# Fewer TensorE instructions in a cross-covariance attention kernel: one transpose for V of two units, fp32 transposes of 128 columns for the logits, grams of two units in the same PSUM banks

## Chip, cores, metric

One core of one Trainium2 chip. Times are device microseconds (us) of one execution; a profile belongs to one execution and gives its span, which is about 1.7 us shorter than the time reported for the same run. Every comparison uses runs of the fast state (a run counts as slow when it is more than 1.5% above the fastest of the same kernel) unless the text says otherwise. Ratios are the mean time of one kernel's fast runs over the mean of the other's fast runs of the same rounds, so they are not quite the ratio of the medians that are quoted beside them; intervals are 95%.

## The reference

```python
# Q, K, V: (8 batches, 12 heads, 512 rows, 64 columns), float32
Q_norm = Q / (np.linalg.norm(Q, axis=-2, keepdims=True) + 1e-10)
K_norm = K / (np.linalg.norm(K, axis=-2, keepdims=True) + 1e-10)
attn = np.einsum('bhnd,bhne->bhde', Q_norm, K_norm)          # 64 x 64 a head
attn = np.exp(attn - np.max(attn, axis=-1, keepdims=True))
attn = attn / (np.sum(attn, axis=-1, keepdims=True) + 1e-10)
return np.einsum('bhnd,bhde->bhne', V, attn)
```

37.75 MB are read and 12.58 MB written.

## The kernel before

Four heads are a *unit*: 128 partitions, 32 for each head, with 16 rows of 64 columns in each partition. There are 24 units and 12 *pairs* of units. A unit's Q and K stand side by side as bf16; one product of this tile with itself (the *gram*, 64 matmuls) gives K^T Q and, on its diagonal, the squares of all norms. V is transposed on TensorE, copied to SBUF, and multiplied with the normalised exponentials. A planner in the program (`Order`) decides the order in which the pieces are issued; all engines then work through their queues in that order.

```python
def cast_v(eng, u):
    vb[u] = vbp.tile([128, T, D], BF16, name="vb")            # one tile a unit
    copy(eng, vb[u], v32[u])

def grams(u):
    g = gram[u] = ps_g.tile([128, HU, 512], F32, name="gram") # four banks, one unit
    for t in range(T):                                        # T = 16
        for h in range(HU):                                   # HU = 4
            x = qkb[u][32 * h:32 * (h + 1), t, :]
            nc.tensor.matmul(g[:, h, 0:2 * D], x, x, start=(t == 0), stop=(t == T - 1))

def powers(s):                                                # pair s
    # ... r8 = (sums of squares) ** -0.5 on GpSimd
    nc.gpsimd.tensor_tensor(
        out=t_, in0=kq[s], in1=r8[s][:, HU:, None].to_broadcast([128, HU, D]), op=ALU.mult)

def logits(s):
    l = lg[s] = ps_l.tile([128, HU, D], F32, name="lg")
    for h in range(HU):
        nc.tensor.matmul(l[LO, h, :], kqs[s][HI, h, :], eye2[HI])   # fp32
        nc.tensor.matmul(l[HI, h, :], kqs[s][LO, h, :], eye2[LO])

def vtrans(s, k, c):
    # ...
            for j in range(J // 2):
                for r in range(2):                            # two units, 64 columns each
                    t = J * c + k * (J // 2) + j
                    nc.tensor.transpose(ps[r * D:(r + 1) * D, n, j, :], vb[2 * s + r][:, t, :], identb)
# (cuts: loads, casts of Q and K, squares, exponentials, normalising, outputs, stores, the planner)
```

## Time and profile before

| kernel before | |
|---|---|
| time, median of the first 3 runs | 134.86 us (134.47 to 135.57) |
| span of the profiled run | 133.4 us |
| busy: TensorE, VectorE, ScalarE, GpSimd | 80.8, 88.3, 73.2, 52.5 us |
| weight loads and matmuls in the trace, each counted as one *record* | 2496 of each, 4992 records, 416 a pair |
| packets of the queue "instruction" (q8) | 19 of 16,384 bytes |
| last gram starts | 114.36 us |

Read it like this: no engine is busy for more than two thirds of the span, so no engine's work as such is the bound. The last gram is the piece to watch, because everything that is still to be stored for the last pair follows from it.

### The profile page before, as it was taken

The numbers are of one execution on the slowest core, as the hardware profiler recorded it, in microseconds if no ns is written. First come the engines' busy times: TensorE is split into PE (matmuls) and PEld (weight loads), VectorE is DVE, ScalarE is ACT, GpSimd is POOL, SyncE is SP. The second block draws the span as 40 slices with busy tenths as digits, with TensorE's granted clock in tenths as the row PEclk, the third lists the DMA queues.
The fourth block names the chain that finished last, engine by engine and source line by source line (L and its number), as shares of the span: only waits on it lengthen the run. The fifth ranks groups of instructions, "written<-read, shape, count | busy, mean of one in ns | idle before, by whom it ended". The sixth has DMA issues, their size and how long they took to land.

```text
span 133.4 us, 5692 instructions
## 1 busy us (share of the span) xinstructions
PE 80.8 (61%) x2496; PEld 68.3 (51%) x2496; DVE 88.3 (66%) x168; ACT 73.2 (55%) x182; POOL 52.5 (39%) x51
## 2 busy tenths in 40 slices
PE   0135557976384859355987926458845586597530
PEld 0134446865283747244966825357734465486420
DVE  2466468799847788583758476485996956596900
ACT  3011107487744819491948777472965648388860
POOL 3003735823838709109306572025058009118000
PEclk9999999999958689996557999777799869869995
DMA  4999999999999999999999999999999999865865
GB/s 141 407 414 418 408 407 407 412 405 407 405 412 404 405 412 412 401 415 407 412 412 409 414 412 417 405 411 417 408 418 407 415 402 419 315 252 201 330 236 193
DMA packets 17192, 50.69 MB, mean 380 GB/s; under 512 B 1552, under 2 KB 2064, under 8 KB 17168
## 3 DMA queue, kind: packets, MB, share of 16 engines
q1 hardware_dynamic: 17168, 50.34, 95.5%
q8 instruction: 19, 0.31, 0.9%
q14 instruction: 5, 0.04, 0.1%
HBM read 37.75 MB, written 12.58 MB: 377 GB/s over the span
## 4 chain that ended last, share of the span: by engine, by line
PE 33%; issue 18%; DVE 17%; POOL 11%; DMA 9%; ACT 6%; SPq 3%; DVEq 0%; POOLq 0%; ACTq 0%
PE gram L172 18%; DMA qk<-in_K_dram 9%; POOL r L200 7%; DVE scr L180 6%; PE po L255 6%; PE lg L209 4%; PE vps L240 4%; DVE n L195 3%; DVE qkb L160 3%; POOL kqs L202 3%; SPq L145 2%; DVE ab L225 2%; ACT vt L135 2%; ACT so L135 2%; ACT kq L135 1%
## 5 line engine op out<-in xcount | busy, mean ns | idle before, releaser
L172 PE MATMUL gram<-qkb 32*128 32x128 bf16 x1536 | 37.2, 258 | 31.1 <-DVE qkb L160 15.4
L172 PEld LDWEIGHTS <-qkb 32*128 32x128 bf16 x1536 | 30.5, 115 | 36.5 <-DVE qkb L160 18.4
L200 POOL TENSOR_TENSOR r<-n,mhalf 128x8 f32<-128x8 f32 x12 | 23.2, 1934 | 48.0 <-DVE n L195 48.0
L160 DVE CAST qkb<-qk 128x1024 bf16<-128x1024 f32 x48 | 35.6, 773 | 7.4 <-DMA qk<-in_Q_dram 4.0
L180 DVE SCALAR_TENSOR_TENSOR scr<-gram,eye 64x256 f32<-64x256 f32 x48 | 20.3, 422 | 19.1 <-ACT kq L135 15.6
L135 ACT COPY vt<-vps 128x1024 bf16<-128x1024 bf16 (+1 forms) x24 | 29.1, 1224 | 4.0 <-PE vps L240 4.0
L135 ACT COPY so<-po 128x512 f32<-128x512 f32 x43 | 23.5, 591 | 12.0 <-PE po L255 11.6
L139 POOL TENSOR_SCALAR vb<-v 128x1024 bf16<-128x1024 f32 x18 | 20.2, 1126 | 21.0 <-DMA v<-in_V_dram 17.4
L255 PE MATMUL po<-ab,vt 128*64 128x128 bf16 x384 | 19.7, 248 | 6.3 <-ACT vt L135 3.4
L135 ACT COPY kq<-gram 64x256 f32<-64x256 f32 x18 | 6.6, 366 | 30.7 <-PE gram L172 23.8
L240 PE MATMUL vps<-identb,vb 128*64 128x128 bf16 x384 | 20.0, 263 | 3.0 <-issue 3.0
L255 PEld LDWEIGHTS <-vt 128*64 128x64 bf16 x384 | 14.4, 125 | 10.3 <-issue 5.0
L216 ACT ACTIVATE ex<-lg,r 128x64 f32<-128x64 f32 x48 | 14.5, 314 | 8.4 <-PE lg L210 8.3
L240 PEld LDWEIGHTS <-vb 128*64 128x64 bf16 x384 | 16.7, 140 | 3.9 <-issue 3.6
L210 PE MATMUL lg<-eye,kqs 64*64 64x64 f32 x96 | 10.1, 254 | 3.6 <-issue 3.6
L209 PE MATMUL lg<-eye,kqs 64*64 64x64 f32 x96 | 10.0, 255 | 3.6 <-POOL kqs L202 3.6
L225 DVE TENSOR_TENSOR ab<-ex,rinv 64x256 bf16<-64x256 f32 x24 | 11.2, 468 | 0.6
L209 PEld LDWEIGHTS lg<-eye,kqs 64*64 64x64 f32 x96 | 8.0, 160 | 5.4 <-POOL kqs L202 4.5
L210 PEld LDWEIGHTS lg<-eye,kqs 64*64 64x64 f32 x96 | 8.1, 161 | 3.9 <-issue 3.9
L216 ACT ACTIVATION_READ_ACCUMULATOR ex<-lg,r 128x1 f32 x48 | 9.8, 205 | 0.0
L195 DVE TENSOR_REDUCE n<-scr 128x8 f32<-128x512 f32 x12 | 8.2, 686 | 0.6
L202 POOL TENSOR_TENSOR kqs<-kq,r 128x256 f32<-128x256 f32 x12 | 8.1, 672 | 0.9
(16 smaller groups left out, 18.4 us busy)
## 6 DMA issues: line engine op xcount, KB each, us to landing
qk<-in_Q_dram SPq DMA_DIRECT2D x24, 512.0 KB, 10.0
qk<-in_K_dram SPq DMA_DIRECT2D x24, 512.0 KB, 10.1
v<-in_V_dram SPq DMA_DIRECT2D x24, 512.0 KB, 10.1
out_dram<-so SPq DMA_DIRECT2D x23, 512.0 KB, 10.0
out_dram<-so SPq DMA_DIRECT2D x2, 256.0 KB, 3.1
```

Of the source, the lines that this page charges most:

```text
L135: nc.scalar.copy(o, i)
L139: nc.gpsimd.tensor_scalar(out=o, in0=i, scalar1=1.0, scalar2=0.0, op0=ALU.mult, op1=ALU.add)
L160: nc.vector.tensor_copy(qkb[u][:, :, y * D:(y + 1) * D], qk32[u][:, y])
L172: nc.tensor.matmul(g[:, h, 0:2 * D], x, x, start=(t == 0), stop=(t == T - 1))
L180: nc.vector.scalar_tensor_tensor(out=scr[s][half, HU * n:HU * n + HU], in0=gram[u][half, :, half], scalar=1e-20, in1=eye2[half, None, :].t ...
L200: nc.gpsimd.tensor_tensor(out=t_, in0=n2, in1=mhalf, op=ALU.pow)
L209: nc.tensor.matmul(l[LO, h, :], kqs[s][HI, h, :], eye2[HI])
L210: nc.tensor.matmul(l[HI, h, :], kqs[s][LO, h, :], eye2[LO])
L216: nc.scalar.activation(e[:, h, :], lg[s][:, h, :], AF.Exp, scale=r8[s][:, h:h + 1], accum_out=z[:, h:h + 1])
L225: nc.vector.tensor_tensor(out=a[half, :, half], in0=e[half], in1=ri[half, :, None].to_broadcast([D, HU, D]), op=ALU.mult,)
L240: nc.tensor.transpose(ps[r * D:(r + 1) * D, n, j, :], vb[2 * s + r][:, t, :], identb)
L255: nc.tensor.matmul(po[s, x][e * D:(e + 1) * D, j].rearrange("p r d -> p (r d)"), w, ab[s][:, h, :])
```

## The change

The intent is fewer TensorE instructions for the same work: V of two units is cast into one tile and turned by one transpose of 128 columns; the grams of both units of a pair share four banks, so that squares and K^T Q of a pair are taken out with half as many, twice as wide instructions; and the logits come from four fp32 transposes of 128 columns in place of eight products with an identity. With that come other placements (the scaling of K on VectorE in 8 of 12 pairs, all V casts on GpSimd) and a planner that counts blocks of 256 TensorE instructions.

```diff
 def cast_v(eng, u):
-    vb[u] = vbp.tile([128, T, D], BF16, name="vb")
-    copy(eng, vb[u], v32[u])
+    if r == 0:
+        vb[s] = vbp.tile([128, T, 2, D], BF16, name="vb")
+    copy(eng, vb[s][:, :, r], v32[u])

 def grams(u):
-    g = gram[u] = ps_g.tile([128, HU, 512], F32, name="gram")
+    if r == 0:
+        gram[s] = ps_g.tile([128, HU, 2, 2, 2 * D], F32, name="gram")
 ...
-            nc.tensor.matmul(g[:, h, 0:2 * D], x, x, ...)
+            nc.tensor.matmul(gram[s][:, h, r, 0], x, x, ...)

+def scale_k(eng, s):
+    kqs[s] = small.tile([128, 2 * HU, D], F32, name="kqs")
+    (nc.vector if eng == "DVE" else nc.gpsimd).tensor_tensor(
+        out=kqs[s][HI], in0=kq[s][HI], in1=r8[s][HI, :, None].to_broadcast([D, 2 * HU, D]), op=ALU.mult)
+
+def scales_q(s):
+    rq[s] = small.tile([128, HU], F32, name="rq")
+    nc.vector.tensor_copy(rq[s][LO], r8[s][LO, 0::2])
+    nc.vector.tensor_copy(rq[s][HI], r8[s][LO, 1::2])

 def logits(s):
-        nc.tensor.matmul(l[LO, h, :], kqs[s][HI, h, :], eye2[HI])
-        nc.tensor.matmul(l[HI, h, :], kqs[s][LO, h, :], eye2[LO])
+        nc.tensor.transpose(l[:, h, :], kqs[s][HI, 2 * h:2 * h + 2].rearrange("p r d -> p (r d)"), eye2[HI])

 def vtrans(s, k, c):
-                for r in range(2):
-                    t = J * c + k * (J // 2) + j
-                    nc.tensor.transpose(ps[r * D:(r + 1) * D, n, j, :], vb[2 * s + r][:, t, :], identb)
+                t = J * c + k * (J // 2) + j
+                nc.tensor.transpose(ps[:, n, j, :], vb[s][:, t].rearrange("p r d -> p (r d)"), identb)
# cut: squares and cross for a pair at once; in the planner, a pause at each block of 256
# TensorE instructions, other costs, ranks and biases
```

More of the change, by code (lines that the diff above doesn't have):

```diff
@@ L21, with __init__ @@
 class Order:
-    HOP = 0.15
-    SLACK = 0.25
+    HOP = 0.10
+    SLACK = 0.1
     QUEUE = 8
     FLIGHT = 2.0
-    def __init__(self):
+    CHUNK, FETCH, FIRST = 256, 6.1, 190
+    def __init__(self, size):
         self.pieces = {}
+        self.size = size
     def add(self, key, engines, after, behind, rank, emit):
@@ L39, in add, with pause @@
         self.pieces[key] = (engines, after, behind, rank, emit)
+    def pause(self, begin, cost, n, done):
+        k0, k1 = (self.count - self.FIRST) // self.CHUNK, (self.count + n - self.FIRST) // self.CHUNK
+        wait = 0.0
+        if k1 > k0 and k1 >= 0:
+            at = begin + cost * (self.FIRST + self.CHUNK * k1 - self.count) / n
+            wait = max(0.0, self.last + self.FETCH - at)
+            if done:
+                self.last = at + wait
+        if done:
+            self.count += n
+        return wait
     def run(self):
         end, begun, free, landed, order = {}, {}, {}, [], []
+        self.count, self.last = 0, -9.0
+        engines_of = {k: p[0] for k, p in self.pieces.items()}
         todo = dict(self.pieces)
@@ L58, in run @@
                     else:
-                        bias = 0.0
-                        if isinstance(cost, tuple):
-                            cost, bias = cost
+                        cost, bias = cost if isinstance(cost, tuple) else (cost, 0.0)
+                        if eng == "PE":
+                            cost += self.pause(begin, cost, self.size(key), False)
                         done = busy = begin + cost
@@ L74, in run @@
                 landed.append(done)
+            if eng == "PE":
+                cost = engines_of[key]["PE"]
+                self.pause(begin, cost, self.size(key), True)
             order.append((begin, len(order), key, eng))
@@ L107 @@
     ctx.enter_context(tc.manual_schedule())
-    NB = dict(qk=6, v=5, vb=4, qkb=3, vt=4, so=10, sm=2, ab=3)
+    NB = dict(qk=6, v=5, vb=4, qkb=3, vt=3, so=10, sm=2, ab=3)
     const = ctx.enter_context(tc.tile_pool(name="const", bufs=1))
@@ L129, in late_pool @@
         return late["p"]
-    qk32, v32, vb, qkb, gram, scr, kq, r8, kqs, lg, ex, ab, vps, vt, po, so = ({} for _ in range(16))
+    qk32, v32, vb, qkb, gram, scr, kq, n2, r8, kqs, rq, lg, ex, ab, vps, vt, po, so = ({} for _ in range(18))
     def copy(eng, o, i):
@@ L144, in load_qk @@
             qk32[u] = qp.tile([128, 2, T, D], F32, name="qk32")
-        nc.sync.dma_start(out=qk32[u][:, x ^ (u % 2)], in_=(Qu, Ku)[x][u * 128:(u + 1) * 128])
+        nc.sync.dma_start(out=qk32[u][:, x], in_=(Qu, Ku)[x][u * 128:(u + 1) * 128])
     def load_v(u):
@@ L158, in cast_qk @@
             qkb[u] = qkp.tile([128, T, 2 * D], BF16, name="qkb")
-        y = x ^ (u % 2)
-        nc.vector.tensor_copy(qkb[u][:, :, y * D:(y + 1) * D], qk32[u][:, y])
+        nc.vector.tensor_copy(qkb[u][:, :, x * D:(x + 1) * D], qk32[u][:, x])
     def cast_v(eng, u):
-        vb[u] = vbp.tile([128, T, D], BF16, name="vb")
-        copy(eng, vb[u], v32[u])
+        s, r = divmod(u, 2)
+        if r == 0:
+            vb[s] = vbp.tile([128, T, 2, D], BF16, name="vb")
+        copy(eng, vb[s][:, :, r], v32[u])
     def grams(u):
-        g = gram[u] = ps_g.tile([128, HU, 512], F32, name="gram")
+        s, r = divmod(u, 2)
+        if r == 0:
+            gram[s] = ps_g.tile([128, HU, 2, 2, 2 * D], F32, name="gram")
         for t in range(T):
@@ L171, in grams, with squares @@
                 x = qkb[u][32 * h:32 * (h + 1), t, :]
-                nc.tensor.matmul(g[:, h, 0:2 * D], x, x, start=(t == 0), stop=(t == T - 1))
-    def squares(u, n):
-        s, r = divmod(u, 2)
-        if (r, n) == (0, 0):
+                nc.tensor.matmul(gram[s][:, h, r, 0], x, x, start=(t == 0), stop=(t == T - 1))
+    def squares(s, n):
+        if n == 0:
             scr[s] = small.tile([128, 2 * HU, D], F32, name="scr")
-        half = (LO, HI)[n ^ r]
+        half = (LO, HI)[n]
         nc.vector.scalar_tensor_tensor(
-            out=scr[s][half, HU * n:HU * n + HU], in0=gram[u][half, :, half], scalar=1e-20,
-            in1=eye2[half, None, :].to_broadcast([D, HU, D]), op0=ALU.add, op1=ALU.mult,
-        )
@@ L185, in cross @@
-    def cross(eng, u):
-        s, r = divmod(u, 2)
-        if r == 0:
-            kq[s] = small.tile([128, HU, D], F32, name="kq")
-        k, q = (HI, LO) if r == 0 else (LO, HI)
-        copy(eng, kq[s][k], gram[u][k, :, q])
+            out=scr[s][half], in0=gram[s][half, :, :, 0, half].rearrange("p h r d -> p (h r) d"), scalar=1e-20,
+            in1=eye2[half, None, :].to_broadcast([D, 2 * HU, D]), op0=ALU.add, op1=ALU.mult,
+        )
+    def cross(eng, s):
+        kq[s] = small.tile([128, 2 * HU, D], F32, name="kq")
+        copy(eng, kq[s][HI], gram[s][HI, :, :, 0, LO].rearrange("p h r d -> p (h r) d"))
@@ L193, in sums @@
     def sums(s):
-        n2 = r8[s] = small.tile([128, 2 * HU], F32, name="n2")
-        nc.vector.tensor_reduce(out=n2, in_=scr[s], axis=mybir.AxisListType.X, op=ALU.add)
+        n2[s] = small.tile([128, 2 * HU], F32, name="n2")
+        nc.vector.tensor_reduce(out=n2[s], in_=scr[s], axis=mybir.AxisListType.X, op=ALU.add)
     def powers(s):
-        n2 = r8[s]
-        t_ = r8[s] = small.tile([128, 2 * HU], F32, name="r8")
-        nc.gpsimd.tensor_tensor(out=t_, in0=n2, in1=mhalf, op=ALU.pow)
@@ L201, in powers @@
-        t_ = kqs[s] = small.tile([128, HU, D], F32, name="kqs")
-        nc.gpsimd.tensor_tensor(
-            out=t_, in0=kq[s], in1=r8[s][:, HU:, None].to_broadcast([128, HU, D]), op=ALU.mult,
-        )
+        r8[s] = small.tile([128, 2 * HU], F32, name="r8")
+        nc.gpsimd.tensor_tensor(out=r8[s], in0=n2[s], in1=mhalf, op=ALU.pow)
+    def scale_k(eng, s):
+        kqs[s] = small.tile([128, 2 * HU, D], F32, name="kqs")
+        (nc.vector if eng == "DVE" else nc.gpsimd).tensor_tensor(
+            out=kqs[s][HI], in0=kq[s][HI], in1=r8[s][HI, :, None].to_broadcast([D, 2 * HU, D]), op=ALU.mult,
+        )
@@ L215, in exps @@
         for h in range(HU):
-            nc.scalar.activation(e[:, h, :], lg[s][:, h, :], AF.Exp, scale=r8[s][:, h:h + 1], accum_out=z[:, h:h + 1])
+            nc.scalar.activation(e[:, h, :], lg[s][:, h, :], AF.Exp, scale=rq[s][:, h:h + 1], accum_out=z[:, h:h + 1])
         ex[s] = (e, z)
@@ L277, with size @@
         abs_.append(a)
-    plan = Order()
+    def size(key):
+        return 8 if key[0] == "vt" and key[-1] is not None else {"gr": 128, "lg": 8, "vt": 16, "ou": 16}[key[0]]
+    plan = Order(size)
     X = 1.29
-    KQ_BIAS, CV_BIAS, VC_BIAS, OC_BIAS, CQ_RANK = 0.3, 0.2, 0.3, 0.2, 2.5
+    SC_BIAS, GR_RANK = -0.6, 1
+    KQ_BIAS, CV_BIAS, VC_BIAS, OC_BIAS, CQ_RANK = 1, 5, 0, 1, 1.5
     QK_PACE, V_FROM, V_PACE, ST_LAG = 0.76, 0.08, 0.8, 0.3
@@ L290, in piece @@
     def piece(key, engines, after, behind, rank, fn, *args):
-        if key[0] in ("cv", "vc", "oc", "kq"):
+        if key[0] in ("cv", "vc", "oc", "kq", "sc"):
             plan.add(key, engines, after, behind, rank, lambda eng: fn(eng, *args))
@@ L306 @@
         piece(("cq", u, 1), {"DVE": 0.72}, [("lk", u)], [("cq", u, 0)], CQ_RANK + 0.001 * u, cast_qk, u, 1)
-        piece(("gr", u), {"PE": 1.75}, [("cq", u, 0), ("cq", u, 1), back("sq", u, 1), back("sa", u, 1)], [], 2, grams, u)
-        piece(("sa", u), {"DVE": 0.43}, [("gr", u), back("rd", s, NB["sm"])], [back("sq", u, 1)], 1, squares, u, 0)
-        piece(("kq", u), {"ACT": 0.43, "DVE": (0.43, KQ_BIAS)}, [("gr", u), back("sc", s, NB["sm"])], [back("kq", u, 1)], 0.9, cross, u)
-        piece(("sq", u), {"DVE": 0.43}, [("kq", u)], [("sa", u)], 1, squares, u, 1)
+        piece(("gr", u), {"PE": 1.6}, [("cq", u, 0), ("cq", u, 1), back("kq", s, 1)], [back("gr", u, 1)], GR_RANK, grams, u)
@@ L312 @@
     for s in range(S):
-        piece(("rd", s), {"DVE": 0.69}, [(x, 2 * s + r) for x in ("sa", "sq") for r in range(2)] + [back("sc", s, NB["sm"])], [], 1, sums, s)
-        piece(("sc", s), {"POOL": 2.5}, [("rd", s), ("kq", 2 * s), ("kq", 2 * s + 1), back("lg", s, NB["sm"]), back("ex", s, NB["sm"])], [], 1, powers, s)
-        piece(("lg", s), {"PE": 0.8}, [("sc", s), back("ex", s, 1)], [], 1, logits, s)
-        piece(("ex", s), {"ACT": 2.05}, [("lg", s), back("nm", s, NB["sm"])], [], 1, exps, s)
@@ L317 @@
-        piece(("nm", s), {"DVE": 1.05}, [("ex", s)] + [back("ou", s, NB["ab"], x) for x in range(4)], [], 1, normalise, s)
+        SM = NB["sm"]
+        piece(("sq", s, 0), {"DVE": 0.70}, [("gr", 2 * s), ("gr", 2 * s + 1), back("rd", s, SM)], [], 1, squares, s, 0)
+        piece(("sq", s, 1), {"DVE": 0.70}, [("gr", 2 * s), ("gr", 2 * s + 1)], [("sq", s, 0)], 1, squares, s, 1)
+        piece(("kq", s), {"ACT": 0.60, "DVE": (0.70, KQ_BIAS)}, [("sq", s, 0), ("sq", s, 1), back("sc", s, SM)], [], 0.9, cross, s)
@@ new lines @@
+        piece(("rd", s), {"DVE": 0.69}, [("sq", s, 0), ("sq", s, 1), back("pw", s, SM)], [], 1, sums, s)
+        piece(("pw", s), {"POOL": 1.9}, [("rd", s), back("rq", s, SM), back("sc", s, SM)], [], 1, powers, s)
+        piece(("sc", s), {"POOL": (1.25, SC_BIAS), "DVE": 0.6}, [("pw", s), ("kq", s), back("lg", s, SM)], [], 1, scale_k, s)
+        piece(("rq", s), {"DVE": 0.2}, [("pw", s), back("ex", s, SM)], [], 1.2, scales_q, s)
+        piece(("lg", s), {"PE": 0.35}, [("sc", s), back("ex", s, 1)], [], 0.2, logits, s)
@@ L318 @@
+        piece(("ex", s), {"ACT": 1.30}, [("lg", s), ("rq", s), back("nm", s, NB["sm"])], [], 1, exps, s)
+        piece(("nm", s), {"DVE": 1.08}, [("ex", s)] + [back("ou", s, NB["ab"], x) for x in range(4)], [], 1, normalise, s)
     for v in range(U):
@@ L321 @@
         piece(("cv", v), {"POOL": 1.08, "DVE": (0.72, CV_BIAS)} if s >= BOTH else {"POOL": 1.08},
-              [("lv", v), vt_end(v // 2 - NB["vb"] // 2)], [back("cv", v, 1)], 3 + 0.01 * v, cast_v, v)
+              [("lv", v), vt_end(v // 2 - NB["vb"])], [back("cv", v, 1)], 3 + 0.01 * v, cast_v, v)
     for s in range(S):
@@ L329 @@
             else:
-                wait = [("vc", s - 1, k, c) if s > TAIL else ("sq", U - 1), ("sa", U - 1)]
+                wait = [("vc", s - 1, k, c) if s > TAIL else ("kq", S - 1)]
             order = [("vt", s, *halves[n - 1]) if n else ("vt", s - 1, 1, 1 if s > TAIL else None) if s else None]
-            piece(("vt", s, k, c), {"PE": 0.48 if t else 0.9}, [("cv", 2 * s), ("cv", 2 * s + 1)] + wait, order, 4 + 0.01 * s, vtrans, s, k, c)
+            piece(("vt", s, k, c), {"PE": 0.38 if t else 0.75}, [("cv", 2 * s), ("cv", 2 * s + 1)] + wait, order, 4 + 0.01 * s, vtrans, s, k, c)
             order = [("vc", s, *halves[n - 1])] if n else []
@@ L342 @@
             order = [("ou", s, x - 1) if x else back("ou", s, 1, 3)]
-            piece(("ou", s, x), {"PE": 0.5}, [("vc", s, *h) for h in halves if h[0] == k] + [("nm", s)] + wait, order, 3 + 0.01 * s, outs, s, x)
+            piece(("ou", s, x), {"PE": 0.45}, [("vc", s, *h) for h in halves if h[0] == k] + [("nm", s)] + wait, order, 3 + 0.01 * s, outs, s, x)
             n = 2 * s + i - NB["so"]
```

## The prediction

> **What bounds the kernel now.** I read the page's slices and DMA queues first, then the chain that ended last, then the timeline and the waits of the SyncE queue in the last 30 us.
>
> The DMA rows of the page, 40 slices of 3.33 us:
>
> ```profile
> PE   0135557976384859355987926458845586597530
> DMA  4999999999999999999999999999999999865865
> GB/s 141 407 414 418 408 407 407 412 405 407 405 412 404 405 412 412 401 415 407 412 412 409 414 412 417 405 411 417 408 418 407 415 402 419 315 252 201 330 236 193
> q1 hardware_dynamic: 17168, 50.34, 95.5%
> q8 instruction: 19, 0.31, 0.9%
> ```
>
> From 3 us to 113 us the 16 DMA engines are full (about 410 GB/s); there nothing can be won by making an engine faster. In the last six slices the rate falls to 193 to 330 GB/s: here the queue has room and no store is ready. That is the only place with time to win. All 24 units' loads are issued by 105.3 us; what is left are stores, and they wait:
>
> ```profile
> 106.24 23.63 SPq L154 DMA_DIRECT2D out_dram<-so  x11
> SPq L154 <- ACT so L135: 15.1, 8, 5.6
> ```
>
> Why are they late? The K half of the last unit is issued at 96.11 us and, at the usual 10 us to landing, is there at about 106. Yet its gram product (64 matmuls) runs only here:
>
> ```profile
> 114.36 0.73 PE L172 MATMUL gram<-qkb 32*128 32x128 bf16 x38 [1.32 <-DVE qkb L160]
> 115.65 0.54 PEld L172 LDWEIGHTS <-qkb 32*128 32x128 bf16 x26 [0.74 <-issue]
> ```
>
> So TensorE is about 8 us behind the data. It is not busy all that time (61% of the span). The chain, in order of time, shows what it does instead: it stops within a block of equal matmuls, waiting for nothing the profile can name.
>
> ```profile
> 36.35 0.70 issue
> 37.05 1.56 PE gram L172 x57
> ...
> 41.27 1.98 issue
> 43.25 0.57 PE gram L172 x25
> ...
> 48.13 1.40 issue
> ...
> 53.53 2.20 issue
> ...
> 59.82 1.83 issue
> 61.66 0.93 PE gram L172 x22
> ...
> 83.69 1.81 issue
> 85.50 1.37 PE gram L172 x37
> ```
>
> The restarts are 37.05, 43.25, 49.54, 55.73, 61.66, ... 85.50 us: 48.45 us for 8 steps, **6.06 us each**, and they go on to 115.65 us. I counted the TensorE records (weight load and matmul each as one) before each stop: 958, 1214, 1470, 1726, 1982, 2238, ...: exactly 256 apart. And queue 8, "instruction", carries 19 packets of 16,384 bytes, that is 256 times 64 bytes; their starts in the trace are 21.90, 28.23, 34.46, 40.79, 47.12, 53.24 us and so on, again 6 us apart, each about 1.4 us before a restart. So TensorE is bound by the **supply of its own instructions**: one block of 256 in 6.06 us, because the fetch has to pass through DMA engines that the data keep full. The end of the kernel is bound by this lag, which arises much earlier.
>
> **What the Trainium skill says.** "Runtime: NRT & Kernel Launch", section Instruction fetch mechanics, says that instructions are refilled in blocks of 16 KiB (256 instructions) through a DMA queue that the sequencer drives, and that crossing a block is "mostly hidden". The block size agrees with the 19 packets; "mostly hidden" does not, in a kernel whose DMA engines are full: up to 2.2 us are lost at a block. "Trainium Kernel Development and Optimization", Key Constraints, says that DMAs of all issuing queues share the same 16 engines and interleave, which fits a fetch of 1.0 us that comes only each 6. "FP8 and Floating Point Precision", TensorE Precision Notes, gives four passes for true FP32; this trace shows two records for each of the 96 fp32 logit matmuls (L209 and L210 have x96 each for 48 in the program). "TensorE: Matmul & The Clock Gate", PE-mode transpose, gives about 275 ns for one 128x128 bf16 transpose in a kernel; here L240 has a mean of 263 ns, pipelined to about 53 ns each (16 in 0.85 us in the chain).
>
> **The change part by part.** Records per pair of units (12 pairs), before to after:
> - grams: 128 matmuls, 256 records; unchanged.
> - V: 32 transposes to 16, thus 64 records to 32. Saves 16 x 53 ns = 0.85 us of TensorE too.
> - logits: 16 matmul records with 16 loads, 32, to 4 transposes, 8 records if an fp32 transpose is one pass (16 if two). Sixteen take 1.06 us in the chain (91.83 to 92.89), four about 0.3.
> - outputs: 32 matmuls, 64 records; unchanged.
>
> Sum: 416 to 360 a pair, 4992 to 4320 in all: 672 / 256 = 2.6 blocks, times 6.06 us = **15.9 us less of supply** (13.6 if two passes). A pair needs 416/256 x 6.06 = 9.85 us of supply before and 8.52 after. DMA gives a pair's worth (6 loads and 2 stores, at 1.27 us between issues) in 10.1 us, and in the first 35 us, with loads alone, in 7.6 us. So before, TensorE falls behind in the first third and never regains it; after, it gains about 1.6 us a pair.
>
> Where is it then at the end? Before, record 958 starts at 30.85 us and the last gram is record 4464. After, the last gram starts at record 3944 of its order. If the supply bound it from the same point, that is 30.85 + (3944 - 958)/256 x 6.06 = 101.5 us; the K data land at 106.1 and need a cast (0.77). So the gram starts at about 107 to 108.5, bound by loads: **6 to 7 us earlier**. At unit 12 the same sum gives 53.4 against a landing at 52, so supply and loads are about level from mid-run.
>
> The rest moves little. Both units' grams in one bank: squares 48 x 422 ns = 20.3 us become 24 of 512 columns, about 0.69 each by the 128x512 reduction's row (686 ns): 16.5. Copies of kq: 24 to 12, about 9.1 to 7.1 us (0.59 for 512 columns, by the so row). A gram waits for an evacuation once a pair instead of twice (TensorE waited 6.2 us for scr). The scaling of K has half the lanes and twice the columns: 8 go to VectorE (0.69 each, 5.5 us), 4 stay on GpSimd (about 1.25). V casts all go to GpSimd (24 x 1.126 = 27 us). VectorE: 88.3 - 3.8 - 2.5 + 5.5 + 2.4 (small copies) - 4.1 - 2.6 + 1.4 = about 85 us; ScalarE about 75; GpSimd about 56. None is near the span.
>
> **The sum.** The order of the 97 transfers is the same in both programs, so until 106.24 us nothing can change. From there the packets that remain took 21.3 us of all 16 engines in the old trace; full slices show a busy share of 1.03, so 20.7 us, and the last packet ends at 126.9 us if the DMA never runs dry. Old trace: last packet 131.99, end of span 133.37, so 1.4 us of closing: span 128.3. The median is 1.5 us over the profiled span: **129.8 us is the floor**.
>
> Does it run dry? Last gram ends at about 110; squares 1.4, reduction 0.7, power 1.95, scaling 0.7, logits 0.5, exponentials 1.3, normalising 1.1: 117.7 to 118.5. V of the last unit (issued 104.95) lands at 115.1, is cast by 116.4 and turned and copied by 118.7. Four output products and copies at about 0.7: 121.5 to 122. The other stores, all but 1.05 MB, keep the DMA busy until about 124 (2.7 us before 126.9). So the last stores come 2 us ahead of need, about what a store needs from issue to first data. I add 0.4 us: **130.2 us**.
>
> **Rivals.** (1) The fetch gets slower or the evacuation of a whole pair blocks the grams (one buffer of four banks, refilled only after kq is copied): about 2 us of wait a pair, other TensorE work fills most of it. If not, half the lag stays and the time is 132 to 133. For it: the waits on scr; against it: those are 6.2 us in 133. (2) ScalarE becomes the bound in the tail: it does nearly all output copies (only 1 on VectorE against 5). It had 9.5 us busy of the last 15.4; packed densely that is 1 us or so later: 131. (3) The lag was hidden anyway and the DMA floor rules: no gain. The GB/s row speaks against it, since 8.0 MB take 25.7 us from 106.24 where 20.7 would do.
>
> **Range and chances.** The floor is hard, since nothing in the change lessens bytes or packets: low 129.3. High 132.3, if rival 1 or 2 holds in half. A gain over 2% is anything under 132.2, which needs only half of the recoverable 5 us: 0.88. Within 2%: 0.11. Slower: 0.01.
>
> **What would show it.** Right: queue 8 has 17 packets in place of 19; GB/s stays near 390 to 410 until 123 us; the last gram starts by 109 us; stops at block borders are gone from the last third; logits have 48 matmul records (96 if two passes). Wrong: GB/s drops at 113 us again with the last gram at 112 us or later, or a chain full of ScalarE copies or of waits of gram for kq.

## The result, and the profile after

The kernel after takes **131.52 us** (131.34 to 132.03, 4 runs) beside 135.16 us; the ratio is 0.9742 (0.9689 to 0.9795). Two later runs of the same kernel as a control, on whatever chip the experiments had, gave 0.9756 (0.9720 to 0.9793) and 0.9766 (0.9708 to 0.9823). So it is faster by 2.3 to 2.6%, inside the predicted range, and 1.3 us above the predicted 130.2.

| | before | after |
|---|---|---|
| span of the profiled run, us | 133.4 | 129.8 |
| mean granted TensorE clock | 0.870 | 0.773 |
| busy, us: TensorE | 80.8 | 81.7 |
| VectorE | 88.3 | 96.2 |
| ScalarE | 73.2 | 75.2 |
| GpSimd | 52.5 | 56.2 |
| weight loads and matmuls, records | 4992 | 4320 |
| packets of the queue "instruction" | 19 | 17 |
| last gram starts, us | 114.36 | 110.26 |
| last data packet ends, us | 131.99 | 128.44 |

The slices and queues of the page of the kernel after, in 40 slices of 3.24 us:

```profile
PE   0045392985829835959578999479596555857610
DMA  4999999999999999999999999999999999999892
GB/s 136 375 399 421 408 414 404 409 413 403 410 405 407 405 408 414 402 415 415 409 419 403 415 412 414 413 417 407 416 407 414 413 412 407 409 402 403 346 334 81
q8 instruction: 17, 0.28, 0.8%
```

The DMA row is full until 120 us, where before it broke down at 113. The rest is in the last two and a half slices: the rate is 346 and 334 GB/s before it ends.

The chain that ended last, in order of time, kernel after (start, length, what):

```profile
35.37 2.62 issue
37.99 0.95 PE po L280 x13
...
59.18 2.63 PE gram L196 x128
...
78.67 0.78 issue
...
92.94 1.19 issue
```

One long stop is left, at 35.4 us (record 1214, again a block's edge); the two short ones shown after it lie at no block's edge. The chain leads through VectorE for 34% of the span (17% before) and no longer through a stop at every block. At 59.18 us the grams of two units run straight through, 128 matmuls. I added up, over all block edges, the time between two weight loads beyond 0.35 us: 15.1 us before, 3.6 us after. This count is steadier than the chain: in the two control runs of the kernel after it is 3.4 and 4.7 us, while the chain that ended last goes through DMA transfers for 63 and 35% of the span there, and for 5% here.

TensorE's busy time did not fall, in part because the granted clock was lower in the profile after (0.773 beside 0.870). The V transposes show another part; the timeline of TensorE at full granted clock, one line of the kernel before and one of the kernel after:

```profile
33.03 0.61 PE L240 MATMUL vps<-identb,vb 128*64 128x128 bf16 x16
```

```profile
29.09 0.62 PE L265 MATMUL vps<-identb,vb 128*128 128x128 bf16 x8
```

Sixteen transposes of 64 columns take as long as eight of 128. The single records show how: before, the transposes of the two units start 3 to 4 ns apart and such pairs follow each other every 56 ns, as single transposes of 128 columns do after. Merging them saves instructions and next to no time, which makes the V part of the change a cleaner test of the instruction supply than I had thought.

The tail of the kernel after, from its timeline (start, length, engine, line, operation; in brackets the idle time before it and who ended it):

```profile
105.89 0.69 DVE L178 CAST qkb<-qk 128x1024 bf16<-128x1024 f32 x1
...
106.31 0.31 ACT L242 ACTIVATE ex<-lg,rq 128x64 f32<-128x64 f32 x1 [2.83 <-PE lg L236]
...
107.23 1.30 DVE L156 COPY vt<-vps 128x1024 bf16<-128x1024 bf16 x1 [0.65 <-PE vps L265]
...
108.62 0.85 DVE L251 TENSOR_TENSOR ab<-ex,rinv 64x256 bf16<-64x256 f32 x2
...
109.51 0.70 DVE L178 CAST qkb<-qk 128x1024 bf16<-128x1024 f32 x1
...
110.26 1.80 PE L196 MATMUL gram<-qkb 32*128 32x128 bf16 x64
```

The Q half of the last unit is cast at 105.89, the K half, issued at 95.92 us and, at the usual 10 us, there by 106, only at 109.51: between them stand a V copy and the normalising of pair 10. The V copy waits 0.65 us for its transposes (the exponentials, which begin at 106.31, are done before it ends). From this copy the chain that ended last leads back over the V transposes of pair 9 (106.23) and the logits of pair 10 (105.54) to the scaling of K of pair 10 on VectorE (103.96). The last gram follows at 110.26.

And one operation is twice as long as I had put it. The operations on the tile `kqs`, kernel after (least, median and greatest duration in ns):

```profile
L223 DVE TENSOR_TENSOR kqs<-kq,r x8: 690/1500/1527, 17.2 to 116.1; 64x512 f32<-64x512 f32 x8
L223 POOL TENSOR_TENSOR kqs<-kq,r x4: 1040/1041/1041, 33.4 to 95.8; 64x512 f32<-64x512 f32 x4
```

The scaling of K takes 690 ns on VectorE once, and about 1500 ns seven times. Overlaid with GpSimd, the seven are those that began while GpSimd was in a V cast, as here:

```profile
103.91 1.04 POOL L158 TENSOR_SCALAR vb<-v 128x1024 bf16<-128x1024 f32 x1
103.96 1.52 DVE L223 TENSOR_TENSOR kqs<-kq,r 64x512 f32<-64x512 f32 x1 [0.92 <-POOL r L219]
```

The cast ends at 104.95; 1.52 us are the 0.99 us until then and somewhat over half a microsecond more. The small copies of the scales behave alike: 16 of 24 take 0.16 to 0.17 us, the 8 that begin after a cast or a scaling on GpSimd has begun 0.89 to 0.95 us. The Trainium skill, "SBUF — State Buffer", section Who interferes with whom, says that VectorE and GpSimd share a pair of SBUF ports as an exclusive lock, and that a VectorE instruction with two SBUF inputs contends with a GpSimd instruction that reads SBUF. The two durations of the scaling agree with it.

### The profile page after: what moved, and what is told of

It is laid out like the page before. It is cut to its first block, busy times and chain, and to the rows that moved or that the text cites.

```text
span 129.8 us, 4986 instructions
## 1 busy us (share of the span) xinstructions
PE 81.7 (63%) x2160; PEld 67.1 (52%) x2160; DVE 96.2 (74%) x161; ACT 75.2 (58%) x179; POOL 56.2 (43%) x49
## 4 chain that ended last, share of the span: by engine, by line
DVE 34%; PE 28%; POOL 10%; ACT 9%; issue 7%; DMA 5%; SPq 1%; POOLq 0%; ACTq 0%; DVEq 0%
PE gram L196 14%; POOL r L219 9%; DVE kqs L223 8%; DVE scr L203 7%; DVE qkb L178 7%; PE po L280 6%; PE vps L265 5%; DMA qk<-in_K_dram 5%; DVE n L215 4%; DVE ab L251 4%; ACT so L154 3%; ACT vt L154 3%; PE lg L236 3%; DVE vt L156 2%; ACT ex L242 2%
## 5 line engine op out<-in xcount | busy, mean ns | idle before, releaser
L196 PE MATMUL gram<-qkb 32*128 32x128 bf16 x1536 | 37.5, 270 | 15.5 <-DVE qkb L178 10.1
L158 POOL TENSOR_SCALAR vb<-v 128x1024 bf16<-128x1024 f32 x24 | 28.0, 1167 | 31.6 <-DMA v<-in_V_dram 29.0
L242 ACT ACTIVATE ex<-lg,rq 128x64 f32<-128x64 f32 x48 | 14.4, 314 | 20.9 <-PE lg L236 18.0
L203 DVE SCALAR_TENSOR_TENSOR scr<-gram,eye 64x512 f32<-64x512 f32 x24 | 16.5, 689 | 7.0 <-PE gram L196 6.7
L265 PE MATMUL vps<-identb,vb 128*128 128x128 bf16 x192 | 19.1, 262 | 0.7 <-ACT kq L154 0.7
L265 PEld LDWEIGHTS <-vb 128*128 128x128 bf16 x192 | 14.5, 118 | 3.4 <-issue 2.1
L223 DVE TENSOR_TENSOR kqs<-kq,r 64x512 f32<-64x512 f32 x8 | 11.1, 1386 | 3.7 <-POOL r L219 3.5
L251 DVE TENSOR_TENSOR ab<-ex,rinv 64x256 bf16<-64x256 f32 x24 | 10.9, 453 | 0.7
L236 PE MATMUL lg<-eye,kqs 64*128 64x64 f32 x48 | 7.0, 284 | 5.5 <-DVE kqs L223 5.1
L242 ACT ACTIVATION_READ_ACCUMULATOR ex<-lg,rq 128x1 f32 x48 | 9.8, 205 | 0.0
L236 PEld LDWEIGHTS lg<-eye,kqs 64*128 64x128 f32 x48 | 5.0, 177 | 7.8 <-DVE kqs L223 6.4
L154 ACT COPY kq<-gram 64x512 f32<-64x512 f32 x12 | 7.0, 580 | 2.0 <-DVE scr L203 1.7
## 6 DMA issues: line engine op xcount, KB each, us to landing
qk<-in_Q_dram SPq DMA_DIRECT2D x24, 512.0 KB, 10.1
v<-in_V_dram SPq DMA_DIRECT2D x24, 512.0 KB, 10.1
```

Of the source, the lines that this page charges most:

```text
L154: nc.scalar.copy(o, i)
L158: nc.gpsimd.tensor_scalar(out=o, in0=i, scalar1=1.0, scalar2=0.0, op0=ALU.mult, op1=ALU.add)
L196: nc.tensor.matmul(gram[s][:, h, r, 0], x, x, start=(t == 0), stop=(t == T - 1))
L203: nc.vector.scalar_tensor_tensor(out=scr[s][half], in0=gram[s][half, :, :, 0, half].rearrange("p h r d -> p (h r) d"), scalar=1e-20, in1=e ...
L223: (nc.vector if eng == "DVE" else nc.gpsimd).tensor_tensor(out=kqs[s][HI], in0=kq[s][HI], in1=r8[s][HI, :, None].to_broadcast([D, 2 * HU, ...
L236: nc.tensor.transpose(l[:, h, :], kqs[s][HI, 2 * h:2 * h + 2].rearrange("p r d -> p (r d)"), eye2[HI])
```

## The experiments

**Theory.** The gain comes from fewer instructions to be fetched: TensorE gets a block of 256 in about 6 us, which is a rate of 42 records a microsecond. The kernel before needs more than that while the DMA engines carry loads alone (a pair in 7.6 us, by the prediction, where its 416 records take 9.85 us), and later nearly as much (a pair in 10.1 us), so that it never makes up the lag. **Rivals:** TensorE's time; the pair-wise evacuation of the grams; the new order. A second question is where the 1.3 us are that the kernel after stays above my figure.

### 1. The records given back, with next to no TensorE time: `padded`

```diff
 def grams(u):   # kernel after
         gram[s] = ps_g.tile([128, HU, 2, 2, 2 * D], F32, name="gram")
+    for n in range(14):
+        x = qkb[u][32 * (n % 4):32 * (n % 4 + 1), 0, :]
+        nc.tensor.matmul(gram[s][:, n % 4, r, 1, 0:1], x, x[:, 0:1], start=True, stop=True)
```

> The kernel after, with 14 extra matmuls of one column in front of each unit's gram, written to a corner of PSUM that nobody reads: 672 records more, so 4992 as in the kernel before, at next to no TensorE work; the order on the other engines is the same. Theory (instruction supply, one block of 256 in 6.06 us): the last gram stands at record 4588 in place of 3944, so from the stop at record 1214 (37.99 us) it can start at 37.99 + 3374/256 x 6.06 = 117.9 us in place of 110.3; 19 blocks are fetched, stops stand at every 256th record; time 135 to 138 us. Rival (the gain is TensorE time, fewer evacuations of the grams or the new order of work): 336 short matmuls are about 10 us of TensorE spread over 130, most of it in its idle time; time 131.5 to 132.2 us.

Measured: 142.97 us, ratio to the kernel before 1.0545 (1.0472 to 1.0618). 19 blocks are fetched, from the fourth to the eighteenth in 85.5 us, 6.1 us each. The last gram starts at 123.15 us. The direction is the theory's, by more than I expected (11.5 us against 3.5 to 6.5): the rival's 131.5 to 132.2 is out. The slices of this run:

```profile
GB/s 170 353 395 419 411 407 411 413 399 409 409 404 410 407 415 404 414 411 413 412 408 418 411 414 411 408 415 408 420 409 409 411 333 268 27 3 287 160 234 211
```

And from its timelines of TensorE and VectorE (the brackets show the wait):

```profile
110.28 0.28 PE L199 MATMUL gram<-qkb 32*128 32x128 bf16 x5 [2.91 <-issue]
110.60 0.68 DVE L206 SCALAR_TENSOR_TENSOR scr<-gram,eye 64x512 f32<-64x512 f32 x1 [4.59 <-PE gram L199]
...
115.81 1.52 DVE L226 TENSOR_TENSOR kqs<-kq,r 64x512 f32<-64x512 f32 x1 [0.92 <-POOL r L222]
```

A stop falls five matmuls before the end of the second gram of pair 10; VectorE stands still for 4.59 us, and everything of pairs 10 and 11 follows later. The sum of supply had put the last gram at 117.9; the other 5 us come from such stops in the middle of work that another engine waits for. That is read from the trace, not isolated by a run. The DMA engines are nearly dry from 120 to 127 us (27 and 3 GB/s in two slices of 3.53 us).

### 2. One part alone: `v_merged_alone`

```diff
 # kernel before, with cast_v and vtrans of the kernel after and nothing else
 # (the V tiles are twice as large, so their pool has half as many buffers)
+    vb[s] = vbp.tile([128, T, 2, D], BF16, name="vb");  copy(eng, vb[s][:, :, r], v32[u])
+    nc.tensor.transpose(ps[:, n, j, :], vb[s][:, t].rearrange("p r d -> p (r d)"), identb)
```

> The kernel before with one part of the change alone: V of two units in one tile and turned by one transpose. 4608 records in place of 4992; order, evacuations, logits and scheduling are the old ones. Theory (supply): the last gram stands at record 4112, so it could start at 30.85 + 3154/256 x 6.06 = 105.5 us, before its data are there; nearly the whole gain comes: 131 to 132.5 us. Rival (the grams in shared banks, the short logits or the new order made the gain): 134 us or more.

Measured: 132.40 us, ratio **0.9764** (0.9695 to 0.9834). The V part alone brings what the whole change brings (0.9742 to 0.9766). Neither the shared banks nor the short logits nor the new order are needed for it. TensorE's busy time is 81.1 us, not less than before, at nearly the same granted clock (0.884 beside 0.870).

The time came out as expected, the path not in full. The supply would have let the last gram start at 105.5 us; it started at 111.76, right behind the logits of the pair before, which waited 1.48 us for GpSimd's scaling of K. From its timeline of TensorE, and its page:

```profile
111.15 0.27 PE L211 MATMUL lg<-eye,kqs 64*64 64x64 f32 x1 [1.48 <-POOL kqs L204]
...
111.76 1.07 PE L174 MATMUL gram<-qkb 32*128 32x128 bf16 x62
q8 instruction: 18, 0.29, 0.9%
```

### 3. The same, with its records given back: `v_merged_padded`

```diff
 # v_merged_alone
+    for n in range(8):                 # 8 x 24 units x 2 records = 384
+        x = qkb[u][32 * (n % 4):32 * (n % 4 + 1), 0, :]
+        nc.tensor.matmul(g[:, n % 4, 256:257], x, x[:, 0:1], start=True, stop=True)
```

> The run with V merged alone, plus 8 matmuls of one column in front of each unit's gram: 384 records more, so exactly the 4992 of the kernel before, while the 10 us of TensorE time that the merged transposes save stay saved (192 short matmuls give back about 3.4 us). Theory (instruction supply): the gain is gone, 134.5 to 137 us, with stops at every 256th record. Rival (merging helps because TensorE is less busy): it keeps most of its gain, 132.5 to 133.3 us.

Measured: ratio **1.0007** (0.9980 to 1.0035), median of all runs 135.93 us; 19 blocks, from the third to the sixteenth 6.1 us each. The gain is gone: the interval holds 1 (the median of all 43 runs of the kernel before in these rounds is 135.27 us). From its timeline of TensorE, and its page:

```profile
115.17 0.21 PE L173 MATMUL gram<-qkb 32*128 32x1 bf16 x8
115.23 1.06 PE L177 MATMUL gram<-qkb 32*128 32x128 bf16 x64
q8 instruction: 19, 0.31, 0.9%
```

(By the count of stops at block edges the two runs hardly differ, 10.9 and 11.2 us; that sum does not order the runs, the start of the last gram does, 111.76 and 115.23 us.) This run and the one before it decide for the number of records: the transposes, the tiles and the order are those of `v_merged_alone`, and only 192 matmuls of one column, with their weight loads, were added. (That the merged transposes would save 10 us of TensorE time, as the expectation says, is wrong, as shown above; what the short matmuls' time cost has to be judged by the next two runs.)

### 4. TensorE time without records: `wide_grams` and `before_wide`

```diff
 # kernel after; the same edit in the kernel before
-    nc.tensor.matmul(gram[s][:, h, r, 0], x, x, start=(t == 0), stop=(t == T - 1))
+    if t % 2 == 0:   # 256 columns; the second half is never read
+        xx = qkb[u][32 * h:32 * (h + 1), t:t + 2, :].rearrange("p t d -> p (t d)")
+        nc.tensor.matmul(gram[s][:, h, r].rearrange("p a d -> p (a d)"), x, xx, start=(t == 0), stop=False)
+    else:
+        nc.tensor.matmul(gram[s][:, h, r, 0], x, x, start=False, stop=(t == T - 1))
```

> The kernel after, with every second gram matmul streaming 256 columns in place of 128 (the second half goes to a part of the bank that nobody reads): more TensorE time, not one record more. Theory (supply): the time stays at 131.5 us within 0.8. Rival (TensorE time): 768 matmuls last longer, perhaps 15 us of TensorE in all, and the time rises to 133 us or more.

> The kernel before with every second gram matmul streaming 256 columns: more TensorE time, no record more. In the changed kernel the same edit took a gram from 1.6 to 2.4 us and cost some 2 to 3 us in all. Theory (before, TensorE waits for its instructions, so longer matmuls fill the stops): the time stays at 135 us within 0.8. Rival (TensorE time bounds the kernel before): 137 to 138 us, as in the changed kernel or more.

Measured: `wide_grams` 0.9856 (0.9791 to 0.9921) of the kernel before, that is 1.2% over the kernel after by its first ratio, from the 4 of 20 runs that count as fast; all 20 lie between 132.13 and 138.44 us (median 135.31), and why they spread so is open. `before_wide` 1.0100 (1.0062 to 1.0137), from 9 of 20; the medians of all runs, 137.37 and 135.27 us, are 1.6% apart. My expectation of no more than 0.8 us failed for both: TensorE time does cost something, 1.4 us in the kernel before, also while it waits for its instructions. But it is cheap: the grams kept TensorE busy for 45.2 us in `wide_grams` and 37.5 in the kernel after, for 44.4 us in `before_wide` and 37.2 in the kernel before, so 7 to 8 us more for 1 to 1.6%. In `v_merged_padded` each gram starts 0.06 to 0.08 us after the first of its eight short matmuls, 1.7 us in all. By that measure they cost 0.2 to 0.4% of the 2.4% that they took back; the records took the rest.

This is an estimate, since the busy time of the whole engine cannot be compared straight: it is 85.8 us in `v_merged_padded` beside 81.1 in `v_merged_alone`, but at a granted clock of 0.801 beside 0.884. The step from the kernel before to `v_merged_alone` needs no such correction: 384 records fewer, the same busy time at nearly the same clock, 2.4% less time.

### 5. The V part alone undone in the kernel after: `v_split`

```diff
-                nc.tensor.transpose(ps[:, n, j, :], vb[s][:, t].rearrange("p r d -> p (r d)"), identb)
+                for r in range(2):
+                    nc.tensor.transpose(ps[r * D:(r + 1) * D, n, j, :], vb[s][:, t, r], identb)
```

> The kernel after with the V part of the change alone undone (two transposes of 64 columns in place of one of 128, the same order everywhere): 4704 records in place of 4320. Theory (supply of records): before the last gram stand 3944 + 350 = 4294 records, so from the stop at record 1214 (37.99 us) it may start at 37.99 + 3080/256 x 6.06 = 110.9 us, just about where the kernel after has it anyway; with the padded run as the measure (672 records for 11.5 us, 4 us more than the sum said) 384 records cost 2 to 6 us: 134 to 137 us. Rival (TensorE time alone): 10 us of TensorE time more, which by the wide grams (20 us for 2) is 1 us: 132.5 us.

Measured: 132.69 us, ratio 0.9817 (0.9753 to 0.9882), beside 0.9766 of the control in the same rounds. That is half a per cent, and the intervals overlap. My 134 to 137 is refuted; the sum of supply, 110.9 us for the last gram and thus hardly bound, was nearer than the extrapolation from `padded` that I put in its place. The rival's number, 132.5, fits, but not its reason, since there is hardly any TensorE time in it: the busy time of `v_split` is 80.2 us, within the 79.0 to 83.5 us of the three profiles of the kernel after.

Laid side by side, the runs suggest a curve with a knee (two orders of work are mixed in it, and `padded` lies off it). The third column is the supply of one pair, records / 256 x 6.06 us; the DMA engines need about 10.1 us for a pair's six loads and two stores (1.27 us between issues):

| run | records a pair | supply a pair, us | ratio to before |
|---|---|---|---|
| before | 416 | 9.85 | 1 |
| `v_merged_padded` | 416 | 9.85 | 1.0007 |
| `padded` (order of the kernel after) | 416 | 9.85 | 1.0545 |
| `v_split` | 392 | 9.28 | 0.9817 |
| `v_merged_alone` | 384 | 9.09 | 0.9764 |
| after | 360 | 8.52 | 0.9742, 0.9756, 0.9766 |

From 416 to 392 the time falls by 1.8%, from 384 to 360 by nothing that these intervals show. The two parts do not add up, since either of them alone lifts the supply most of the way.

### 6. Fewer bytes in the queue: `half_loads`

```diff
 # kernel before; Q, K and V alike
-        nc.sync.dma_start(out=v32[u], in_=Vu[u * 128:(u + 1) * 128])
+        for i in range(2):
+            p = slice(64 * i, 64 * i + 64)
+            nc.sync.dma_start(out=v32[u][p], in_=Vu[u * 128 + 64 * i:u * 128 + 64 * i + 64])
```

> The kernel before with each load issued as two of 64 partitions: the same bytes in the same packets, but, with eight transfers outstanding, about half the bytes in the queue. If a fetch of instructions stands behind the outstanding bytes of the data, it comes about twice as fast (3 to 4.5 us for a block), the stops shrink and the time falls to 130 to 132 us with no instruction less on TensorE. If a fetch is served packet by packet in turn with the data, whatever is outstanding, the blocks still come each 6 us and the time stays at 135. If the halves use fewer DMA engines, the rate falls and the time rises; then this run says nothing of the fetch.

Measured: 181.13 us (the profile and three of four runs slow; no ratio is made of it). Its slices:

```profile
GB/s 135 231 230 230 232 236 233 239 239 241 236 235 243 244 248 244 247 347 265 312 330 278 335 265 325 313 242 308 246 326 316 334 342 374 376 392 348 402 405 145
```

The rate falls as in the third case of the expectation: loads of 64 partitions run at 230 to 248 GB/s in the first 17 slices in place of 410, so the run says nothing of what a fetch waits for. (The reason was not the expected one: the packets of queue 1 still fill 100.1% of the 16 engines' span.) Blocks came each 7.9 us. That a fetch is slow because the DMA engines are full therefore rests on weaker signs: each fetch is one packet that itself takes 1.0 us, the blocks come each 6 us while the engines are full, and in the kernel before the next-to-last one came 4.5 us after its forerunner, once the rate had fallen. In that kernel the next fetch's packet starts 3.6 to 3.9 us after each restart between 30 and 110 us, but 2.2 and 1.2 us after the last two block edges (115.65 and 122.37 us), when the rate is lower. It is not shown by a run of its own.

### 7. Where the missing 1.3 us are: `tail_swap`, `early_gram`, `early_tail`

`tail_swap` takes three operations of the last pair to other engines:

```diff
 # kernel after, pair 11 only
+    scaling of K: GpSimd, straight after the power     (was VectorE)
+    two copies of the scales: ScalarE                  (was VectorE)
+    both V casts: VectorE                              (was GpSimd)
```

> The kernel after, with three operations of the last pair alone on other engines: the scaling of K on GpSimd straight after the power, the two small copies of the scales on ScalarE, the two V casts on VectorE. Theory (the 1.3 us that the kernel after stays above my 130.2 are VectorE operations held up by GpSimd's casts: the scaling 1.42 us in place of 0.69, a small copy 0.89 in place of 0.16): the exponentials of the last pair start at about 117.5 in place of 118.7 us, the V casts end at 117.5 in place of 118.4, and the time falls by 0.7 to 1.2 us, to 130.3 to 130.8. Rival (the end is set by the DMA alone, or by ScalarE's copies): within 0.3 us of the control.

Measured: 131.99 us, ratio 0.9763 (0.9721 to 0.9805), beside 131.96 us and 0.9756 for the control of the same rounds. No gain: the rival's case. Its profile fell in the slow state, so I don't read steps from it. The longer scaling and copies of the last pair are real, but taking them off VectorE in this way wins nothing; whether the V casts, now on VectorE, took back what was won, this run cannot tell.

`early_gram` and `early_tail` change the order in which the pieces are issued:

```diff
 # kernel after; a piece is moved to stand right behind another
+    early_gram:  cast of K 23 behind cast of Q 23; gram 23 behind the first V transposes of pair 9;
+                 one V copy of pair 9 on ScalarE
+    early_tail:  the same, and of pair 11: scaling behind the power, scales behind it,
+                 logits behind the V transposes of pair 10, exponentials behind its V copies
```

> The kernel after with the last K cast placed straight behind the last Q cast on VectorE, the last gram in front of the output products of pair 9 on TensorE, and one V copy of pair 9 on ScalarE. Theory (the last gram starts at 110.3 us in place of my 107 to 108.5 because its cast stands in line behind a V copy and a normalising that wait for the exponentials of pair 10): it starts by 107.5 us in a fast run; but the scaling of K of the last pair still stands behind the V copies of pair 10, so the time falls by 0.3 us at most. Rival (the last gram sets the end): it falls by 1 us or more.

> As early_gram, and the scaling of K, the scales, the logits and the exponentials of the last pair moved in front of the copies of pair 10. Theory (what is missing to 130.2 us is the line in which the last pair's short operations stand): the exponentials of the last pair are done by 116.5 us in place of 119.9, GpSimd's V casts come before 116.2, the DMA engines stay full to 124 us, and the time is 130 to 131 us. Rival (pair 10's outputs, now later, leave the DMA engines dry in their place): no gain or a loss.

Measured: control 131.94 us, 0.9766; `early_gram` 131.61 us, **0.9738** (0.9685 to 0.9790); `early_tail` 132.53 us, 0.9784 (0.9726 to 0.9842). In `early_gram` the last gram starts at 107.88 us, 2.4 us before the kernel after's, and the time is 0.3 us under the control's, within the noise, as the expectation said: an earlier last gram alone did not move the end. (The V copy moved to ScalarE was not isolated from it.) The trace of `early_gram` shows what stayed behind:

```profile
114.00 0.58 ACT L154 COPY kq<-gram 64x512 f32<-64x512 f32 x1
...
114.64 1.86 PE L265 MATMUL vps<-identb,vb 128*128 128x128 bf16 x16 [0.68 <-ACT kq L154]
...
115.33 1.51 DVE L156 COPY vt<-vps 128x512 bf16<-128x512 bf16 x2 [3.39 <-PE vps L265]
```

The copy of kq of the last pair stands behind V and output copies in ScalarE's line and starts at 114.00 us, not earlier than in the kernel after (113.60), although its gram ended 2.3 us earlier. The V transposes of pair 10 wait for it, and VectorE stands still for 3.39 us. In `early_tail`, where 130 to 131 us were expected, from its timeline:

```profile
108.57 1.86 PE L196 MATMUL gram<-qkb 32*128 32x128 bf16 x64
...
114.97 1.28 DVE L223 TENSOR_TENSOR kqs<-kq,r 64x512 f32<-64x512 f32 x1 [2.36 <-ACT kq L154]
```

The scaling of K, now in front, waits 2.36 us for the same copy of kq (114.28 us in this run); nothing is won. I did not get a version that is clearly faster than the kernel after. What remains above the floor looks like a line of short operations on three engines where each move meets the next wait; which one binds in the unmoved kernel is left open. The copy of kq is the first candidate, and no run moved it.

One view that all profiled runs share, from their traces:

| run | last gram starts, us | span, us | from there to the end |
|---|---|---|---|
| before | 114.36 | 133.4 | 19.0 |
| `before_wide` | 115.08 | 134.8 | 19.7 |
| `v_merged_padded` | 115.23 | 133.3 | 18.1 |
| `padded` | 123.15 | 141.3 | 18.2 |
| `v_split` | 113.53 | 131.7 | 18.2 |
| `v_merged_alone` | 111.76 | 130.7 | 18.9 |
| `wide_grams` | 112.67 | 132.0 | 19.3 |
| after, and its controls | 110.26, 112.31, 109.88 | 129.8, 131.2, 129.7 | 19.5, 18.9, 19.8 |
| `early_tail` | 108.57 | 130.8 | 22.2 |
| `early_gram` | 107.88 | 130.2 | 22.3 |

(`tail_swap` is left out for its state, `half_loads` for its rate.) Where the last gram comes at 109.9 us or later, the end follows it by 18 to 20 us, whatever made it late; brought forward by hand to 108, it did not move the end in these two runs.

## Why the prediction was right, and where it was off

- **The bound.** Right. With 384 records given back and little else (1.7 us of short matmuls) the gain of the V part vanishes (0.9764 to 1.0007). Why a fetch takes 6 us stays argued.
- **"Their starts ... each about 1.4 us before a restart."** Misread: the packets start 2.3 to 2.6 us before a restart and end 1.2 to 1.6 us before it. The spacing, on which the sum rests, is as stated.
- **The number of records.** Right: 4320, with 48 weight loads and 48 matmuls for the 48 fp32 transposes, thus two records each; 17 blocks. The fetch stayed at 6 us for a block wherever TensorE was short of instructions.
- **"Saves 16 x 53 ns = 0.85 us of TensorE too."** Wrong. Sixteen transposes of 64 columns take 0.61 us at full clock, eight of 128 take 0.62; TensorE's busy time went from 80.8 to 81.7 us. The four fp32 transposes of a pair, put at 0.3 us, take 0.47 to 0.69 us in the chain.
- **The knee.** Setting 9.85 and 8.52 us against 10.1 us a pair was right as a rate at which the early lag is made up. It also says that 9.1 would nearly do, and I did not draw this: most of the change was not needed for the time.
- **"The gram starts at about 107 to 108.5, bound by loads."** Off by some 2 us: 110.26. The sum took a cast of 0.77 us after landing; in the queue of VectorE that cast stood behind a V copy, which waited for transposes issued behind the logits of pair 10, and a normalising. Instruction supply was not what held it (there is no stop at the edges next to it). Nor was the lead there from mid-run: the gram of unit 12, for which the sum gave 53.4 us, started at 59.12 us, as in the kernel before (59.09).
- **"VectorE ... about 85 us."** Wrong, 96.2. The scaling of K was put at 0.69 us and took 1.39 on average (8 x 0.70 = 5.6 us), the small copies at 0.1 and took 0.41 and 0.42 (24 x 0.32 = 7.6 us). The rest was about right. I had not asked what GpSimd does at that moment. But taking these off VectorE in the last pair (`tail_swap`) won nothing.
- **"The last stores come 2 us ahead of need."** This is the step that cost the 1.3 us. Both of its lines ran late: the normalising of the last pair ended at 121.1 us and not at 117.7 to 118.5, the last V copy at 121.85 and not at 118.7. So the last output copy ended at 124.57 us and not at 121.5 to 122, and the DMA engines ran partly dry from 120 us on; the last packet ended at 128.44 in place of 126.9. (That 2 us is about what a store needs from issue to first data is not what a trace shows: in the kernel before a store issued at 120.78 us moved its first packet at 121.67, the DMA engines being idle from 121.18 on.)
- **What would show it.** Three of the five signs came: 17 packets, no stop at a block's edge in the last third (at most 0.1 us between two weight loads), 48 matmul records. Two did not: GB/s held until 120 us and not 123, and the last gram started at 110.26 us and not by 109. The gram's 4.1 us in place of 6 to 7 cost little time, since `early_gram`, with 2.4 us more, is not clearly faster: as far as that run can tell, it is luck that this miss did not show in the time.
- **Rival 3** (no gain, the DMA floor rules) is out by the gain itself; the rate held until 120 us. **Rival 1** (evacuation of a whole pair blocks the grams) would have shown in waits of the gram for kq; there is one in the kernel after, 3.5 us. **Rival 2** (ScalarE in the tail): its busy time is 4.0 us of the last 9.8; no run shows it as the bound. But its line does delay the tail: in the kernel after, the chain that ended last passes two output copies and the copy of kq on ScalarE (112.44 to 114.19 us), and `early_gram` and `early_tail` wait for that copy. So this rival is not settled.

## What to carry to other kernels

Count the instructions of an engine that is neither busy nor waiting for anything named: if its stops are exactly 256 instructions apart, it is short of instructions, and the remedy is fewer of them, even if they do not get shorter. Compare the supply (blocks of 256 times their measured spacing) with the time that the real bound gives a unit of work. To be just below that is not enough when a lag has to be made up: here 9.85 us against 10.1 was too slow, 9.1 to 9.3 brought most of the gain, and cuts beyond that brought nothing that these runs show. And before a piece is moved to another engine, look at what shares its path: an operation of 0.69 us became 1.5 beside a neighbour's cast.

## What the Trainium skill lacked or had wrong

- "Runtime: NRT & Kernel Launch", section Instruction fetch mechanics: the block of 256 instructions is right; "mostly hidden" is not in this case. Here, with the DMA engines full, a block came each 6.06 us, stops reached 2.2 us by the chain of waits (2.5 us between two weight loads), 15.1 us in all, and giving back 384 records, with 1.7 us of short matmuls, cost 2.4% (0.9764 to 1.0007).
- No page that I read gives the spacing of such blocks under DMA load, or the test for it: stops in TensorE that are 256 records apart.
- "FP8 and Floating Point Precision", section TensorE Precision Notes: four passes for true FP32, but not how they appear in a trace. The fp32 products with an identity show two matmul records each (96 for 48 on each of two lines), the fp32 transposes one (48 for 48); how many passes a record stands for, no run shows.
- "TensorE: Matmul & The Clock Gate", section PE-mode transpose: about 275 ns for one is near the row mean of the transposes of 128 columns (262 ns); but that section gives no figure for a row of them: their records overlap, and eight in a row took 0.62 us, 56 ns from one to the next.
- "SBUF — State Buffer", section Who interferes with whom, was right: the scaling with two SBUF inputs took 0.69 us alone and 1.41 to 1.53 beside a GpSimd cast.
